# One scan chain over the chunks for all channel groups, and all states copied out at once

## The chip, the cores and the metric

One core of a Trainium2 chip. The metric is the device time of one execution in microseconds (us). A run gives the time of an execution; one execution is also taken by the hardware profiler, which lists the instructions of the five engines (TensorE, VectorE, ScalarE, GpSimd, SyncE) and the DMA transfers.

## What is computed

One layer of a backbone over 1024 latent tokens and 256 context tokens, width 1024. A mixer runs two groups of channels side by side, an output projection joins them, and a squared-ReLU MLP follows; both are post-normalised. The change lies in the second group of the mixer, the S5 part:

```python
def run(u, h0):
    bu = jnp.einsum('blgh,gph->blgp', u.astype(jnp.complex64), b_bar)
    a = jnp.broadcast_to(lam_bar, (1, u.shape[1]) + lam_bar.shape)
    h, h_fin = linear_scan(a, bu, h0, reverse)
    return jnp.einsum('blgp,ghp->blgh', h, c_mat).real, h_fin
h0 = jnp.zeros((u_ctx.shape[0], S5_GROUPS, S5_STATE), jnp.complex64)
y_ctx, h_fin = run(u_ctx, h0)
y_lat, _ = run(u_lat, h_fin)
```

64 groups of 16 channels each drive 64 complex diagonal states, forwards and backwards; the scan over the latent tokens starts from the last state of the context. A skip, a Gelu and a gated linear unit (GLU, `g * sigmoid(g @ w + b)`) follow.

## The kernel before

Tokens are taken in chunks of 8, so there are 32 chunks of context and 128 of latent tokens (`CC` = 32, `NCH` = 160), and the scan runs over chunks. Inside a chunk everything is matmuls with prepared operands. The 64 groups stand in eight channel tiles m = 0 to 7 of eight groups.

`s5_in` (line 590) makes the chunks' inputs to the scan: per group two matmuls on TensorE into PSUM, and copies of the result into the state tile, H0 for tiles 0 to 3 and H1 for tiles 4 to 7 (128 partitions x 160 chunks x real and imaginary x 32 groups). Partitions 0 to 63 hold the forward direction (line 603, ScalarE), 64 to 127 the backward one with the chunks reversed, in two copies for context and latent chunks (lines 605 and 606: VectorE for m < 4, ScalarE for the others).

`scan` (line 608), called for one half at a time, works on VectorE. It first brings the 32 context chunks together in five levels of a tree (tile sC), and then goes through 127 steps, one latent chunk after the other. A step has three instructions, all on line 47, a helper: sT (both products, 128 elements per partition), sU (their sum, 64) and the addition into H (64). Each needs the one before.

`s5_states` copies a tile's states, out of H in the order that the matmuls want, into h2: forwards on ScalarE (line 724), backwards on ScalarE for m < 4 and on VectorE for the others (line 725). When the four tiles of a half are copied, G0 or G1, the input of the GLU, takes the memory of H0 or H1. `s5_out` then does, per tile, 24 matmuls into two PSUM banks (lines 751 to 753, tile ps_so, two buffers), a Gelu on ScalarE (line 754, tile gs), eight transposes (ps_gt) and a split of the result into a high and a low part in G (line 762 ScalarE, line 763 VectorE through line 47). It loads mt, u2 and yf. The GLU's products (ps_gl) of the first two output tiles run along with it.

Between `s5_in` and `s5_out` TensorE has other work, which needs no scan: the gate projections `proj_gate` (ps_mm, evicted by a Gelu into ge) and the first half of the output projection (ps_wo). Their weights come as fp32 and are split on the way into a high part wh (ScalarE, line 98) and a low part wl (VectorE, line 47); the same is done to some of the inputs mh (mix_in).

The order of the instructions on each engine isn't the order of the code. A scheduler places them by its own costs of engines and transfers; each engine then works through its list in order, waiting where an operand isn't there. So the scan steps of both halves, weight splits and gate products are interleaved on VectorE.

Of the kernel before, what the change touches and what calls it, by code (L numbers as in the profile page):

```python
# [15 lines left out]
P = 128  # L16
# [25 lines left out]
def build(nc, tc, a, out):  # L42
# [541 lines left out]
    hp_ = [pool("h0", side="right", stack=hst)]  # L584
    sc = pool("sc", side="right", stack=hst)
    hp_.append(pool("h1", side="right", stack=hst))
    H = [p.tile([P, NCH, 2, GH], F32, tag="h", name=f"H{i}", bufs=1) for i, p in enumerate(hp_)]
# [4 lines left out]
    def s5_in(m):  # L592
        ub = inp.tile([P, 8, NCH], F32, tag="ub", name="ub", bufs=2)
        ld(ub, uscr[m].rearrange("t (c g) n -> (t c) g n", g=8))
        for q in range(2):
            xt = inp.tile([P, 4, 2, P], F32, tag="xt", name="xt", bufs=3)
            in_ld[m] = ld(xt, xscr[m, q])
            for g in range(4):
# [5 lines left out]
                cp = V.tensor_copy if m < 4 else S.copy  # L604
                cp(hv[64:128, :, 0:CC], ps[64:128, :, CC - 1::-1])
                cp(hv[64:128, :, CC:NCH], ps[64:128, :, NCH - 1:CC - 1:-1])

    def scan(hf):
        h = H[hf]
        hs = slice(hf * GH, (hf + 1) * GH)  # L610

# [10 lines left out]
        al = sc.tile([P, 2, 2, GH], F32, tag=f"al{hf}", name=f"al{hf}", bufs=1)  # L622
        V.tensor_copy(al[:, 0], a8[:, 0, 0:1, hs].to_broadcast([P, 2, GH]))
        V.tensor_copy(al[:, 1], a8[:, 0, 1:3, hs])
        for i in range(CC, NCH - 1):
            t = sc.tile([P, 2, 2, GH], F32, tag=f"sT{hf}", name="sT", bufs=2)
            tt(t, al, h[:, i - 1:i].to_broadcast([P, 2, 2, GH]), MUL)
            u = sc.tile([P, 2, GH], F32, tag=f"sU{hf}", name="sU", bufs=2)
            tt(u, t[:, 0], t[:, 1, ::-1, :], ADD)
            tt(h[:, i], u, h[:, i], ADD)  # L630
# [14 lines left out]
    for hf in range(2):  # L645
        for m in range(4):
            s5_in(4 * hf + m)
    inst.close()
    for m in range(8):
        proj_gate(m)  # L650
# [78 lines left out]
    def s5_states(m):  # L729
        h2 = h2s[m] = sop[m % 4 // 3].tile([P, 8, 2, CL], F32, tag="h2", name="h2", bufs=3 if m % 4 < 3 else 1)  # L730
        for q in range(2):
            starts(H[m // 4], h2[:, 4 * q:4 * q + 4], (m % 4) * 8 + 4 * q, V.tensor_copy if m >= 4 else S.copy)

    def s5_out(m):
        if m % 2 == 0:
            mtt[m // 2] = sop[1].tile([P, 16, P], F32, tag="mt", name="mt", bufs=2)
            kv = kpscr[m // 2].rearrange("m (g c) x -> c (m g) x", g=8)
            for t in range(T8):
                ld(mtt[m // 2][16 * t:16 * t + 16], kv[:, :, (8 - t) * 16:(8 - t) * 16 + P])
        mt = mtt[m // 2][:, 8 * (m % 2):8 * (m % 2) + 8]  # L740
# [24 lines left out]
    for hf in range(2):  # L765
        if hf == 0:
            scan(0)
# [696 lines left out]
```

## Time and profile before

| | us |
|---|---|
| runs: 1600.06, 1594.12, 1595.54; median | 1595.54 |
| profiled execution, its time | 1594.69 |
| its span in the trace | 1592.9 |
| TensorE (PE) busy | 1476.7 (93%) |
| VectorE (DVE) busy | 1256.8 (79%) |
| ScalarE (ACT) busy | 843.0 (53%) |
| scan steps sT, 254 on VectorE, mean 0.286 | 66.9 busy |

Busy times are sums over the whole span; an engine that is 79% busy can still be the one waited for in a stretch. Times in the rows are counted from the start of the span. A row of a timeline shows start and length of an instruction (or of several of one kind that follow each other, with their number), engine, line, what is written and what it is made from, and in brackets how long the engine had been idle before, and what ended that idle time. Instructions of one engine may overlap in part, so the distance between two starts, and not the length, tells what an instruction costs its engine.

### The profile page before, as it was taken

To read this page: it belongs to the slowest core of one execution; us is meant where nothing else is said; L and a number is where in the kernel's file an instruction comes from. 1 tells how busy PE (TensorE), PEld (TensorE's weight loads), DVE (VectorE), ACT (ScalarE), POOL (GpSimd) and SP (SyncE) were. 2 spreads that over 40 slices of the span, in tenths; PEclk is the share of its full clock that TensorE was granted. 3 is DMA by queue.
4 is the path that set the end of the run, shared out by engine and by line. 5 is a ranking of instruction groups with operands and counts; after the bars stand their busy time and mean duration, and the time that the engine had idled before them with its cause. 6 is when DMAs were issued, how large, how long until landed. Compare 5 with 4: busy or idle time off the path is not lost. (4 is left out here: it accounts for less than half of the span.)

```text
span 1592.9 us, 20440 instructions
## 1 busy us (share of the span) xinstructions
PE 1476.7 (93%) x7148; PEld 1202.4 (75%) x7148; DVE 1256.8 (79%) x2555; ACT 843.0 (53%) x1178; POOL 71.0 (4%) x141
## 2 busy tenths in 40 slices
PE   7899998999978999699999799989899899999997
PEld 2687777778756878598878677867788788888886
DVE  7899999998866989635978789778787566667877
ACT  4675656666795331954233576444555554344425
POOL 0000000000000000000000011111111000000000
PEclk9999999999999999799999999999999999999999
DMA  7623323323664752983768576777764786776703
GB/s 255 233 94 119 115 99 120 105 106 119 231 215 137 209 183 91 264 201 119 228 207 265 173 242 232 279 248 268 245 219 167 268 287 215 263 251 210 240 7 106
DMA packets 131382, 304.16 MB, mean 191 GB/s; under 512 B 16208, under 2 KB 47440, under 8 KB 129872
## 3 DMA queue, kind: packets, MB, share of 16 engines
q1 hardware_dynamic: 104048, 237.45, 46.9%
q0 software_dynamic: 13184, 47.72, 8.4%
q10 hardware_dynamic: 14048, 17.70, 3.1%
q8 instruction: 56, 0.92, 0.2%
q14 instruction: 46, 0.38, 0.1%
HBM read 219.52 MB, written 83.30 MB: 190 GB/s over the span
## 5 line engine op out<-in xcount | busy, mean ns | idle before, releaser
L98 ACT CAST wh<-wr 128x1024 fp32r<-128x1024 f32 x113 | 118.4, 1051 | 230.0 <-PE ps_m L1276 73.8
L47 DVE TENSOR_TENSOR wl<-wr,wh 128x1024 fp32r<-128x1024 f32 (+1 forms) x161 | 170.5, 1060 | 83.7 <-ACT wh L98 77.2
L1066 PE MATMUL ps_m<-xt,wh 128*128 128x512 f32 x512 | 160.7, 395 | 0.0
L1276 PE MATMUL ps_m<-bh,wh 128*128 128x512 f32 x392 | 153.7, 392 | 3.8 <-ACT bh L1238 3.7
L1276 PE MATMUL ps_m<-bl,wh 128*128 128x512 f32 x392 | 153.4, 391 | 0.5 <-DVE bl L47 0.5
L1276 PE MATMUL ps_m<-bh,wl 128*128 128x512 f32 x392 | 153.3, 391 | 0.0
L380 PE MATMUL ps_mm<-x0h,wh 128*128 128x512 f32 x352 | 140.3, 399 | 1.0 <-ACT wh L98 1.0
L380 PE MATMUL ps_mm<-x0h,wl 128*128 128x512 f32 x352 | 140.0, 399 | 0.9 <-DVE wl L47 0.9
L380 PE MATMUL ps_mm<-x0l,wh 128*128 128x512 f32 x352 | 140.0, 398 | 0.0
L1066 PEld LDWEIGHTS ps_m<-xt,wh 128*128 128x128 f32 x512 | 97.5, 191 | 21.2 <-issue 0.3
L1066 PE MATMUL ps_m<-xt,wl 128*128 128x512 f32 x256 | 101.9, 398 | 10.5 <-DVE wl L47 10.5
L1276 PEld LDWEIGHTS ps_m<-bh,wh 128*128 128x128 f32 x392 | 73.8, 188 | 20.6 <-ACT bh L1238 4.1
L1276 PEld LDWEIGHTS ps_m<-bl,wh 128*128 128x128 f32 x392 | 74.0, 189 | 16.6 <-DVE bl L47 1.0
L1276 PEld LDWEIGHTS ps_m<-bh,wl 128*128 128x128 f32 x392 | 74.0, 189 | 15.5
L675 PE MATMUL ps_wo<-ms,wh 128*128 128x512 f32 x256 | 81.7, 400 | 2.7 <-ACT ms L799 2.7
L1066 PE MATMUL ps_m<-x,wh 128*128 128x512 f32 x256 | 81.8, 400 | 1.0 <-ACT wh L1149 1.0
L380 PEld LDWEIGHTS ps_mm<-x0h,wl 128*128 128x128 f32 x352 | 67.2, 191 | 14.3 <-DVE wl L47 1.4
L380 PEld LDWEIGHTS ps_mm<-x0h,wh 128*128 128x128 f32 x352 | 67.1, 191 | 13.5 <-ACT wh L98 1.4
L380 PEld LDWEIGHTS ps_mm<-x0l,wh 128*128 128x128 f32 x352 | 67.1, 191 | 12.5
L47 DVE TENSOR_TENSOR sT<-al,H 128x128 f32<-128x128 f32 x254 | 66.9, 286 | 1.3
L1066 PEld LDWEIGHTS ps_m<-xt,wl 128*128 128x128 f32 x256 | 49.0, 191 | 23.6 <-DVE wl L47 13.4
L47 DVE TENSOR_TENSOR bl<-br,bh 128x1024 fp32r<-128x1024 f32 x49 | 59.5, 1218 | 2.2 <-ACT bh L1238 2.2
(352 smaller groups left out, 3696.2 us busy)
## 6 DMA issues: line engine op xcount, KB each, us to landing
wr<-in_w SPq DMA_DIRECT2D x79, 512.0 KB, 5.2
br<-hq SPq DMA_DIRECT2D x49, 512.0 KB, 5.0
mo<-in_ada_t SPq DMA_DIRECT2D x32, 512.0 KB, 4.1
hq<-hs POOLq DMA_DIRECT2D x14, 1024.0 KB, 8.2
wr<-in_w_in SPq DMA_DIRECT2D x24, 512.0 KB, 4.3
wr<-in_w_out SPq DMA_DIRECT2D x24, 512.0 KB, 4.5
xt<-xt ACTq DMA_DIRECT2D x16, 512.0 KB, 2.7
yd<-Y SPq DMA_DIRECT2D x16, 512.0 KB, 2.6
```

What stands on the lines that cost most here:

```text
L47: (eng or V).tensor_tensor(out=o, in0=x, in1=y, op=op)
L98: S.copy(hi, raw)
L380: PE.matmul(ps, w[:, ks], x, start=(k == 0 and c == 0), stop=(k == KT - 1 and c == 2))
L675: PE.matmul(ps, u[:, ks], v[:, js], start=(c == 0), stop=(c == 3 * KT - 1))
L1066: PE.matmul(ps, u[:, ks], v, start=(first and c == 0), stop=(last and c == 11))
L1276: PE.matmul(pss[m], w[:, 512 * k + P * m:512 * k + P * m + P], x[:, 512 * k:512 * k + 512], start=(q == 0 and k == 0 and c == 0), stop=(q ...
```

## The change

H0 and H1 become one tile H for all 64 groups. The context scan stays apart for each half and is called as soon as that half's inputs are there (`scan_context`). The 127 steps are done once, for both halves in one instruction each: sT has 256 elements per partition, sU and H 128. All eight tiles' states are then copied out, forwards on ScalarE, backwards on VectorE, and one tile G takes the place of H. In `s5_in` the backward copies are shared out in another way. For the memory that this takes, h2 has seven buffers in two pools, and `s5_out` loads mt per tile (it was per two tiles) and u2 and yf per half tile.

```diff
@@ -581,10 +581,10 @@
 
 
     hst, inst = ExitStack(), ExitStack()
-    hp_ = [pool("h0", side="right", stack=hst)]
+    hp_ = pool("h", side="right", stack=hst)
     sc = pool("sc", side="right", stack=hst)
-    hp_.append(pool("h1", side="right", stack=hst))
-    H = [p.tile([P, NCH, 2, GH], F32, tag="h", name=f"H{i}", bufs=1) for i, p in enumerate(hp_)]
+    HA = hp_.tile([P, 2, NCH, 2, GH], F32, tag="h", name="H", bufs=1)
+    H = [HA[:, i] for i in range(2)]
     inp = pool("inp", stack=inst)
 
     last_in, in_ld = {}, {}
@@ -601,14 +601,13 @@
                     last_in[m] = PE.matmul(ps[:, i, :], xt[:, g, i, :], ub[:, 4 * q + g, :], start=True, stop=True)
                 hv = H[m // 4].rearrange("p s r g -> p r s g")[:, :, :, (m % 4) * 8 + 4 * q + g]
                 S.copy(hv[0:64], ps[0:64])
-                cp = V.tensor_copy if m < 4 else S.copy
-                cp(hv[64:128, :, 0:CC], ps[64:128, :, CC - 1::-1])
-                cp(hv[64:128, :, CC:NCH], ps[64:128, :, NCH - 1:CC - 1:-1])
-
-    def scan(hf):
+                (V.tensor_copy if g % 2 else S.copy)(hv[64:128, :, 0:CC], ps[64:128, :, CC - 1::-1])
+                V.tensor_copy(hv[64:128, :, CC:NCH], ps[64:128, :, NCH - 1:CC - 1:-1])
+
+    def scan_context(hf):
+
         h = H[hf]
         hs = slice(hf * GH, (hf + 1) * GH)
-
         for q in range(5):
             d = 1 << q
             for o in range(0, CC, 16 * d):
@@ -619,15 +618,22 @@
                 tt(t[1], a8[:, q, 1:3, hs].unsqueeze(1).to_broadcast([P, n, 2, GH]), lo, MUL)
                 tt(hi, t[0], hi, ADD)
                 tt(hi, t[1][:, :, ::-1, :], hi, ADD)
-        al = sc.tile([P, 2, 2, GH], F32, tag=f"al{hf}", name=f"al{hf}", bufs=1)
-        V.tensor_copy(al[:, 0], a8[:, 0, 0:1, hs].to_broadcast([P, 2, GH]))
-        V.tensor_copy(al[:, 1], a8[:, 0, 1:3, hs])
+
+    def scan():
+
+        al = sc.tile([P, 2, 2, 2, GH], F32, tag="al", name="al", bufs=1)
+        for hf in range(2):
+            hs = slice(hf * GH, (hf + 1) * GH)
+            V.tensor_copy(al[:, 0, hf], a8[:, 0, 0:1, hs].to_broadcast([P, 2, GH]))
+            V.tensor_copy(al[:, 1, hf], a8[:, 0, 1:3, hs])
+        h = HA.rearrange("p f s r g -> p s f (r g)")
+        al = al.rearrange("p i f r g -> p i f (r g)")
         for i in range(CC, NCH - 1):
-            t = sc.tile([P, 2, 2, GH], F32, tag=f"sT{hf}", name="sT", bufs=2)
-            tt(t, al, h[:, i - 1:i].to_broadcast([P, 2, 2, GH]), MUL)
-            u = sc.tile([P, 2, GH], F32, tag=f"sU{hf}", name="sU", bufs=2)
-            tt(u, t[:, 0], t[:, 1, ::-1, :], ADD)
-            tt(h[:, i], u, h[:, i], ADD)
+            t = sc.tile([P, 2, 2, 2, GH], F32, tag="sT", name="sT", bufs=2)
+            tt(t.rearrange("p i f r g -> p i f (r g)"), al, h[:, i - 1].unsqueeze(1).to_broadcast([P, 2, 2, 2 * GH]), MUL)
+            u = sc.tile([P, 2, 2, GH], F32, tag="sU", name="sU", bufs=2)
+            tt(u, t[:, 0], t[:, 1, :, ::-1, :], ADD)
+            tt(h[:, i], u.rearrange("p f r g -> p f (r g)"), h[:, i], ADD)
 
 
     def proj_gate(m):
@@ -645,7 +651,9 @@
     for hf in range(2):
         for m in range(4):
             s5_in(4 * hf + m)
+        scan_context(hf)
     inst.close()
+    scan()
     for m in range(8):
         proj_gate(m)
     sost, mixst = ExitStack(), ExitStack()
@@ -727,30 +735,28 @@
     mtt, h2s = {}, {}
 
     def s5_states(m):
-        h2 = h2s[m] = sop[m % 4 // 3].tile([P, 8, 2, CL], F32, tag="h2", name="h2", bufs=3 if m % 4 < 3 else 1)
+        h2 = h2s[m] = sop[2 < m < 7].tile([P, 8, 2, CL], F32, tag="h2", name="h2", bufs=4 if 2 < m < 7 else 3)
         for q in range(2):
-            starts(H[m // 4], h2[:, 4 * q:4 * q + 4], (m % 4) * 8 + 4 * q, V.tensor_copy if m >= 4 else S.copy)
+            starts(H[m // 4], h2[:, 4 * q:4 * q + 4], (m % 4) * 8 + 4 * q, V.tensor_copy)
 
     def s5_out(m):
-        if m % 2 == 0:
-            mtt[m // 2] = sop[1].tile([P, 16, P], F32, tag="mt", name="mt", bufs=2)
-            kv = kpscr[m // 2].rearrange("m (g c) x -> c (m g) x", g=8)
-            for t in range(T8):
-                ld(mtt[m // 2][16 * t:16 * t + 16], kv[:, :, (8 - t) * 16:(8 - t) * 16 + P])
-        mt = mtt[m // 2][:, 8 * (m % 2):8 * (m % 2) + 8]
-        u2 = sop[1].tile([P, 8, CL], F32, tag="u2", name="u2", bufs=3)
-        ld(u2, uscr[m].rearrange("t (c g) n -> (t c) g n", g=8)[:, :, CC:NCH])
-        yf = sop[1].tile([P, 2, 2, 4, P], F32, tag="yf", name="yf", bufs=3)
-        ld(yf, yscr[m])
+        mt = sop[1].tile([P, 8, P], F32, tag="mt", name="mt", bufs=2)
+        kv = kpscr[m // 2][m % 2].rearrange("(g c) x -> c g x", g=8)
+        for t in range(T8):
+            ld(mt[16 * t:16 * t + 16], kv[:, :, (8 - t) * 16:(8 - t) * 16 + P])
         h2 = h2s[m]
         gs = sc.tile([P, T8, 8, 16], F32, tag="gs", name="gs", bufs=2)
         for s in range(2):
+            u2 = sop[1].tile([P, 4, CL], F32, tag="u2", name="u2", bufs=3)
+            ld(u2, uscr[m].rearrange("t (c g) n -> (t c) g n", g=8)[:, 4 * s:4 * s + 4, CC:NCH])
+            yf = sop[1].tile([P, 2, 4, P], F32, tag="yf", name="yf", bufs=4)
+            ld(yf, yscr[m][:, s])
             ps = psx.tile([P, 4, P], F32, tag="si", name="ps_so", bufs=2)
             for g in range(4):
                 gl = 4 * s + g
-                PE.matmul(ps[:, g, :], u2[:, gl, :], mt[:, gl, :], start=True, stop=False)
-                PE.matmul(ps[:, g, :], h2[:, gl, 0, :], yf[:, s, 0, g, :], start=False, stop=False)
-                PE.matmul(ps[:, g, :], h2[:, gl, 1, :], yf[:, s, 1, g, :], start=False, stop=True)
+                PE.matmul(ps[:, g, :], u2[:, g, :], mt[:, gl, :], start=True, stop=False)
+                PE.matmul(ps[:, g, :], h2[:, gl, 0, :], yf[:, 0, g, :], start=False, stop=False)
+                PE.matmul(ps[:, g, :], h2[:, gl, 1, :], yf[:, 1, g, :], start=False, stop=True)
             S.activation(gs[:, :, 4 * s:4 * s + 4].rearrange("n t g c -> n g t c"),
                          ps.rearrange("n g (t c) -> n g t c", t=T8), AF.Gelu_apprx_tanh)
         hl = glin[m]
@@ -762,19 +768,14 @@
             S.copy(hl[:, 0, HS[j]], pf)
             tt(hl[:, 1, HS[j]], pf, f(hl[:, 0, HS[j]]), SUB)
 
-    for hf in range(2):
-        if hf == 0:
-            scan(0)
-        for m in range(4 * hf, 4 * hf + 4):
-            s5_states(m)
-        if hf == 0:
-            scan(1)
-
-        g = hp_[hf].tile([P, 5, 2, NL], F32R, tag="h", name=f"G{hf}", bufs=1)
-        for m in range(4):
-            glin[4 * hf + m] = g[:, m]
-        for m in range(4):
-            s5_out(4 * hf + m)
+    for m in range(8):
+        s5_states(m)
+
+    gt = hp_.tile([P, 10, 2, NL], F32R, tag="h", name="G", bufs=1)
+    for m in range(8):
+        glin[m] = gt[:, m]
+    for m in range(8):
+        s5_out(m)
     sost.close()
     zst = ExitStack()
     zp = pool("zp", stack=zst)
```

The orders of the two kernels at three places. Names end in a buffer's number.

ScalarE in `s5_in`, second half of the groups, before:

```order
L603 COPY H1_3775<-ps_si_4043 64x2x160
L605 COPY H1_3775<-ps_si_4043 64x2x32
L606 COPY H1_3775<-ps_si_4043 64x2x128
L603 COPY H1_3775<-ps_si_4053 64x2x160
L605 COPY H1_3775<-ps_si_4053 64x2x32
L606 COPY H1_3775<-ps_si_4053 64x2x128
L603 COPY H1_3775<-ps_si_4059 64x2x160
L605 COPY H1_3775<-ps_si_4059 64x2x32
L606 COPY H1_3775<-ps_si_4059 64x2x128
```

and now:

```order
L603 COPY H_3771<-ps_si_4075 64x2x160
L603 COPY H_3771<-ps_si_4085 64x2x160
L604 COPY H_3771<-ps_si_4085 64x2x32
L98 CAST wh_5124<-wr_5122 128x1024
L642 ACTIVATE ge_5049<-ps_mm_5024 128x512
L603 COPY H_3771<-ps_si_4091 64x2x160
L98 CAST wh_5191<-wr_5189 128x1024
L603 COPY H_3771<-ps_si_4097 64x2x160
L604 COPY H_3771<-ps_si_4097 64x2x32
L603 COPY H_3771<-ps_si_4103 64x2x160
```

The long copy of the backward latent chunks (line 606 before) is no longer in ScalarE's list, and the short one stands behind every second group; two weight splits have come in between.

VectorE in the chain of steps, before, with both halves under way:

```order
L47 TENSOR_TENSOR sT_6131<-al1_6038,H1_3775 128x128
L47 TENSOR_TENSOR sU_5554<-sT_5552 128x64
L47 TENSOR_TENSOR sU_6133<-sT_6131 128x64
L47 TENSOR_TENSOR H0_3774<-sU_5554,H0_3774 128x64
L47 TENSOR_TENSOR H1_3775<-sU_6133,H1_3775 128x64
L47 TENSOR_TENSOR sT_5557<-al0_5344,H0_3774 128x128
L47 TENSOR_TENSOR sT_6136<-al1_6038,H1_3775 128x128
L47 TENSOR_TENSOR sU_5559<-sT_5557 128x64
L47 TENSOR_TENSOR sU_6138<-sT_6136 128x64
```

and now, with a weight split and a gate product between the instructions of two steps:

```order
L47 TENSOR_TENSOR sT_4395<-al_4280,H_3771 128x256
L47 TENSOR_TENSOR wl_5469<-wr_5466,wh_5468 128x1024
L47 TENSOR_TENSOR sU_4397<-sT_4395 128x128
L47 TENSOR_TENSOR ge_5317<-ge_5317 128x512
L47 TENSOR_TENSOR H_3771<-sU_4397,H_3771 128x2x64
L47 TENSOR_TENSOR sT_4400<-al_4280,H_3771 128x256
L47 TENSOR_TENSOR sU_4402<-sT_4400 128x128
L47 TENSOR_TENSOR H_3771<-sU_4402,H_3771 128x2x64
```

Two chains, with an instruction of the other between two of the one, have become one chain of instructions of double length.

ScalarE where the states are copied out and `s5_out` begins, before (H0 first, H1 later):

```order
L724 COPY h2_5997<-H0_3774 64x1024
L725 COPY h2_5997<-H0_3774 64x1024
L724 COPY h2_5997<-H0_3774 64x1024
L725 COPY h2_5997<-H0_3774 64x1024
L98 CAST wh_7228<-wr_7226 128x1024
L754 ACTIVATE gs_6690<-ps_so_6691 128x4x8x16
L754 ACTIVATE gs_6690<-ps_so_6705 128x4x8x16
L724 COPY h2_6883<-H1_3775 64x1024
L762 CAST G0_6676<-ps_gt_6719 128x512
L762 CAST G0_6676<-ps_gt_6726 128x512
L724 COPY h2_6883<-H1_3775 64x1024
L754 ACTIVATE gs_6737<-ps_so_6738 128x4x8x16
```

and now:

```order
L732 COPY h2_6016<-H_3771 64x1024 x2
L732 COPY h2_6021<-H_3771 64x1024 x2
L732 COPY h2_6026<-H_3771 64x1024 x2
L732 COPY h2_6031<-H_3771 64x1024 x2
L732 COPY h2_6036<-H_3771 64x1024 x2
L732 COPY h2_6041<-H_3771 64x1024 x2
L732 COPY h2_6046<-H_3771 64x1024 x2
L732 COPY h2_6051<-H_3771 64x1024 x2
L760 ACTIVATE gs_6066<-ps_so_6071 128x4x8x16
L760 ACTIVATE gs_6066<-ps_so_6089 128x4x8x16
L768 CAST G_6056<-ps_gt_6103 128x512
```

Before, the Gelu of the first tile stood behind the copies of the first half alone, and each copy of the second half behind a Gelu or a split of the first. Now the sixteen copies of all tiles stand in one piece ahead of the first Gelu.

## Rows read from the trace of the kernel before

**Rows 1.** Busy time by windows: engines PE, PEld, DVE, ACT, POOL; clock, DMA.

```profile
661.00:673.86 12.86, 0.00 (x1) 0.00 (x1) 1.75 (x2) 12.75 (x13) 1.13 (x2) 0.63 1.13 325
678.00:740.00 62.00, 62.00 (x466) 57.44 (x465) 18.95 (x24) 29.58 (x37) 0.00 (x0) 1.00 0.65 170
```

**Rows 2.** Waits of TensorE, 417 to 760 us: total, times, longest.

```profile
PE ps_si L601 <- ACT H L606: 13.1, 23, 0.7
PE ps_so L751 <- ACT gs L754: 13.0, 1, 13.0
```

**Rows 3.** Timeline of ScalarE around the copies of H0's states.

```profile
637.14 2.08 ACT L724 COPY h<-H 64x1024 f32<-64x1024 f32 x1 [6.20 <-DVE H L47]
...
670.32 1.92 ACT L725 COPY h<-H 64x1024 f32<-64x1024 f32 x1
672.26 1.04 ACT L98 CAST wh<-wr 128x1024 fp32r<-128x1024 f32 x1
673.21 1.08 ACT L754 ACTIVATE gs<-ps_so 128x512 f32<-128x512 f32 x2
```

**Rows 4.** Timeline: last step of H1's chain on VectorE, TensorE's restart.

```profile
659.45 0.23 DVE L47 TENSOR_TENSOR H<-sU,H 128x64 f32<-128x64 f32 x1
...
673.86 0.80 PE L751 MATMUL ps_so<-mt,u 128*128 128x128 f32 x2 [13.01 <-ACT gs L754]
```

**Rows 5.** Groups by line and shape, 400 to 760 us: busy, mean ns, idle before.

```profile
L47 DVE TENSOR_TENSOR sT<-al,H 128x128 f32<-128x128 f32 x254 | 66.9, 286 | 1.3
L47 DVE TENSOR_TENSOR H<-sU,H 128x64 f32<-128x64 f32 x254 | 49.7, 219 | 1.3
...
L724 ACT COPY h<-H 64x1024 f32<-64x1024 f32 x16 | 32.0, 2003 | 6.3 <-DVE H L47 6.2
...
L47 DVE TENSOR_TENSOR sC<-a,H 128x512 f32<-128x512 f32 x12 | 8.1, 697 | 22.9 <-ACT H L605 22.8
...
L47 DVE TENSOR_TENSOR mh<-mraw,mh 128x1024 fp32r<-128x1024 f32 x3 | 3.7, 1222 | 4.7 <-ACT mh L662 4.7
...
L47 DVE TENSOR_TENSOR H<-sC,H 128x256 f32<-128x256 f32 x4 | 1.7, 417 | 0.0
```

**Rows 6.** Timeline of VectorE: a gate product, and a split between two steps.

```profile
523.09 0.68 DVE L47 TENSOR_TENSOR ge<-ge 128x512 f32<-128x512 f32 x1
...
594.62 1.21 DVE L47 TENSOR_TENSOR wl<-wr,wh 128x1024 fp32r<-128x1024 f32 x1
595.76 0.21 DVE L47 TENSOR_TENSOR sU<-sT 128x64 f32<-128x64 f32 x1
```

**Rows 7.** Timeline of VectorE: copies of the first half, context scan, first step.

```profile
441.04 0.26 DVE L605 COPY H<-ps_si 64x64 f32<-64x64 f32 x1
441.16 0.59 DVE L606 COPY H<-ps_si 64x256 f32<-64x256 f32 x1
441.60 0.27 DVE L605 COPY H<-ps_si 64x64 f32<-64x64 f32 x1
...
445.19 1.34 DVE L47 TENSOR_TENSOR sC<-a,H 128x512 f32<-128x512 f32 x2
...
456.63 0.29 DVE L47 TENSOR_TENSOR sT<-al,H 128x128 f32<-128x128 f32 x1
```

**Rows 8.** Timeline of ScalarE: copies of the second half, beginning and end.

```profile
446.14 0.26 ACT L605 COPY H<-ps_si 64x64 f32<-64x64 f32 x1
446.25 0.60 ACT L606 COPY H<-ps_si 64x256 f32<-64x256 f32 x1
...
447.60 0.26 ACT L605 COPY H<-ps_si 64x64 f32<-64x64 f32 x1
...
491.08 0.63 ACT L606 COPY H<-ps_si 64x256 f32<-64x256 f32 x1
```

**Rows 9.** Timeline of VectorE: steps of one half alone, and in pairs.

```profile
457.48 0.29 DVE L47 TENSOR_TENSOR sT<-al,H 128x128 f32<-128x128 f32 x1
...
458.32 0.29 DVE L47 TENSOR_TENSOR sT<-al,H 128x128 f32<-128x128 f32 x1
...
586.66 0.48 DVE L47 TENSOR_TENSOR sT<-al,H 128x128 f32<-128x128 f32 x2
...
587.61 0.48 DVE L47 TENSOR_TENSOR sT<-al,H 128x128 f32<-128x128 f32 x2
```

**Rows 10.** DMA issues: KB each, median us to landing.

```profile
mt<-kp SPq DMA_DIRECT2D x32, 128.0 KB, 5.7
```

## The prediction

> **What bounds the kernel now.** I read the stretch from 417 to 760 us, where the S5 part lies, by windows first [rows 1]. TensorE is at work in all of 678 to 740 us and in none of 661 to 673.86: the one long hole in this stretch. The waits of TensorE over it [rows 2] name the reason: the first matmul of the second channel tile of s5_out waits 13.0 us for the Gelu of line 754, which must empty its PSUM bank. The ScalarE timeline [rows 3] tells why the Gelu is late. ScalarE copies the states of groups 0 to 31 out of H0, sixteen copies of 2.00 us [rows 5], begun when the chain of H0 ends at 637.1; the last starts at 670.32, the Gelu at 673.21, and TensorE goes on at 673.86 [rows 4]. The chain of H1 ends at 659.7 [rows 4] and holds nobody up: its copies lie between the Gelus of tiles 0 to 3 while TensorE is full. So this stretch ends by: chain of one half, its copies, Gelu. What the change does to 673.86 is what it does to the kernel, since the work behind is the same and TensorE is full there [rows 1].
>
> **The change, part by part.** The orders show it: the first Gelu now stands behind the copies of all eight tiles, and all copies behind the one chain of both halves. So the new time of resumption is: end of the input phase, context scan, chain, sixteen ScalarE copies, Gelu.
>
> *Input phase (s5_in).* The first half ends on VectorE at 445.19 [rows 7]. Of its copies VectorE loses half the short ones; loads and TensorE also held it back, so I take 446. In the second half ScalarE had three copies per group, 1.46 us from one to the next, and ended at 491.7 [rows 8]. It now loses the copy of 0.6 us and half of the short ones: about 0.8 us, 32 groups in 26 us. VectorE is longer now: per group 0.44 us for the long copy and half of 0.12 for the short one [rows 7], 32 x 0.50 = 16.0; in between stands the context scan of the first half, 445.19 to 456.63, 11.4 us; and three weight splits, 1.14 from start to start for a duration of 1.21 [rows 6], and two ge products, 0.60 by the same difference for 0.68 [rows 6]: 4.6. That is 32.0 us. With 2 us for waits between engines the phase ends at 446 + 34 = 480. Bounds: ScalarE alone would allow 472; no gain at all leaves 491.7.
>
> *Context scan of the second half.* 11.4 us again, with three ge and one split among it (2.9): the chain begins at 494.4. Before, VectorE idled 22.8 us in front of it [rows 5]; that idle goes.
>
> *The chain.* Before, a step of one half alone takes 457.48 to 458.32, 0.85 us [rows 9]: three instructions, each waiting for the one before. Two interleaved halves take 586.66 to 587.61, 0.95 us for the pair [rows 9]: the instructions of one half run in the other's latency. The merged step keeps the three waits and doubles the lengths. From 64 to 128 elements an instruction grows by 286 - 219 = 67 ns, from 128 to 256 by 417 - 286 = 131 [rows 5], so the step takes 0.85 + 0.131 + 2 x 0.067 = 1.115 us, and 127 steps 141.6 us. Halving the number of instructions thus buys nothing over the pairs: 0.95 against 1.115. It gains only over the stretches in which one half runs alone, some 14 steps ahead of the context scan of H1 and some 25 at the end.
>
> Among the steps stand 13 weight splits, 3 splits of mix inputs and 9 ge. Between two dependent steps such an instruction costs its own spacing, less the latency that it covers, (2 x 0.85 - 0.95) / 6 = 0.13 us as in the pair: 1.14 - 0.13 = 1.01 and 0.60 - 0.13 = 0.47, together 16.2 + 4.2 = 20.4. The mix splits wait, as before, for inputs that come back through DRAM: 4.7 us [rows 5]. So the chain ends at 494.4 + 141.6 + 20.4 + 4.7 = 661.1, for both halves, 1.4 us behind the old end of H1 and 24 us behind that of H0, the one that counted.
>
> *Copies.* All sixteen on ScalarE now start there: 16 x 2.00 = 32.0 us. VectorE's sixteen, of the same shape, lie beside them. Nothing is left to cover them: by then TensorE has only the first tile's 24 matmuls. With the Gelu and the restart (0.65, from 673.21 to 673.86) TensorE goes on at 693.8.
>
> *What is hidden.* TensorE's gate and output projections can end some 20 us sooner (ahead of the last input matmul stand 54 gate matmuls where 23 stood, and the stalls on ScalarE in the input phase go), but that only lengthens the hole. The weight splits they need stand early enough in the chain, so they add no stall. ScalarE is freed of eight copies between the Gelus behind the hole; TensorE was full there, so that is worth nothing.
>
> *More and smaller loads.* mt, u2 and yf now come in 48 more transfers, with buffers for about two tiles in place of three. A tile takes TensorE 9.4 us (673.9 to 740 for seven); a transfer of mt lands 5.7 us after issue [rows 10]. The first three tiles lie ready during the hole. For the other five I take 0; the upper bound is 2 us each, 10 us; a gain is excluded, since TensorE did not wait for them.
>
> **Sum.** 693.8 - 673.9 = +19.9 us. The profiled execution took 1594.7 us (span 1592.9 and 1.8 around it), 0.9 below the median of 1595.5. 1594.7 + 19.9 = **1615 us**.
>
> **A rule against a row.** The rows give a tensor_tensor 0.219 us at 64 elements and 0.286 at 128 [rows 5]: about 0.15 us fixed, whatever the length. The Trainium skill ("VectorE: DVE Perf Modes", sections on the TRN2 errata and on rules for kernel authors) says that VectorE exposes this latency between instructions, that one large tile pays it once, and advises fewer instructions. It calls for the merge. The pair's 0.95 us [rows 9] disagrees: six instructions with durations of 1.45 us in all lie in it, so between independent ones much of the fixed part is already hidden.
>
> **Rivals.**
> *A, faster: length is free in a waiting chain.* If the wait alone set the step, the merged one would take 0.85 us: 127 x 0.265 = 33.7 us less, TensorE on at 660.1, 1581. For it: the same three waits. Against: the rows on length [rows 5]. It decides (over 0.5%, 8 us, about what a measurement here can tell from no change) below 0.895 us per step.
> *B, same: each instruction pays its fixed part in full and nothing else.* Then a merged step is 0.417 + 2 x 0.286 = 0.99 us with no gap: 16 us less than my chain, 1599. Against: a single step takes 0.85 us [rows 9] for durations of 0.72, so a waiting instruction starts 0.04 us behind the end of the last. This is what the skill's rule of the paragraph above comes to at best.
> *C, slower still: the loads of s5_out set its pace.* With fewer buffers each tile from the fourth on waits some 2 us: 1625. For it: eight mt transfers are issued per tile, not per two. Against: a tile's buffers are free nearly a tile and a half before its successor needs them.
> *D, the input phase gains nothing.* If loads or TensorE hold it, it ends at 491.7 and all moves by 12 us: 1627. For it: the same loads now have to come in less time. Against: up to 491 ScalarE's copies followed each other without a gap [rows 8], and nothing else in that half was full.
>
> **Chances.** Forecast 0.60, A 0.07, B 0.13, C 0.12, D 0.08. Faster by over 0.5%: 0.07 (A). Within 0.5%: 0.14 (B, and the low end of the forecast). Slower: 0.79. Range 1600 to 1627: the low end is the forecast with the input phase at its bound of 472 and no wait of the mix splits (12.7 us less, 1602) and B's neighbourhood; the high end is C and D, each alone. A lies outside, and C with D.
>
> **What would show it.** Right: sT at about 0.42 us and three instructions per 1.10 to 1.13 us; one hole of TensorE of 50 us or more, but for 24 matmuls, that ends near 694 us on the Gelu; sixteen ScalarE copies without a gap from about 661; no idle of VectorE in the input phase. Wrong: steps under 0.95 us, copies that begin before 645, a Gelu between the copies, or new DMA waits in s5_out.

## The result, and the profile after

The changed kernel takes 1636.2 us (median of 4 runs, 1631.8 to 1637.5) where the kernel before took 1594.8: ratio 1.0249, interval 1.0218 to 1.0280. Slower was forecast, but by 20 us and not by 41; the range ended at 1627. The profiled execution took 1635.7 us with a span of 1633.9, 41.0 us more than the span before.

Windows of the changed kernel (columns as in [rows 1]):

```profile
452.00:492.00 40.00, 35.04 (x183) 27.49 (x182) 37.52 (x80) 29.12 (x53) 0.00 (x0) 1.00 0.72 241
...
661.00:678.00 17.00, 3.85 (x18) 3.85 (x19) 15.94 (x36) 5.82 (x4) 0.00 (x0) 0.50 0.00 0
678.00:703.00 25.00, 4.72 (x32) 4.53 (x32) 13.85 (x12) 24.53 (x15) 0.00 (x0) 0.64 0.31 85
...
740.00:778.00 38.00, 34.30 (x251) 30.46 (x250) 5.73 (x9) 9.17 (x17) 0.00 (x0) 1.00 0.60 180
```

The hole of TensorE, 12.86 us before [rows 1], now reaches from 644 to 703 with one tile's matmuls in it, first at a granted clock of 0.50 (1.2 GHz). What is new stands in the last line: in the stretch behind the hole, where TensorE was busy without a break [rows 1], it is idle for 3.7 of 38 us. The waits of TensorE, 400 to 900 us (total, times, longest), name both:

```profile
PE ps_so L758 <- ACT h L732: 29.7, 1, 29.7
PE ps_gt L766 <- ACT gs L760: 24.4, 7, 20.3
PE ps_si L601 <- DVE H L605: 11.1, 8, 7.3
```

The first is the wait for the chain and the first copies; of the second, 20.3 us are the wait for the first Gelu, which answers to the 13.0 us of [rows 2], and the rest is a short wait in six more tiles. The third lies in the input phase, 7.3 us of it at its start. ScalarE's timeline shows where that comes from, and the end of the hole:

```profile
426.00 0.69 ACT L603 COPY H<-ps_si 64x320 f32<-64x320 f32 x1 [4.85 <-DMA hs<-ii]
...
672.18 29.38 ACT L732 COPY h<-H 64x1024 f32<-64x1024 f32 x16 [26.03 <-DVE H L47]
701.46 1.06 ACT L760 ACTIVATE gs<-ps_so 128x512 f32<-128x512 f32 x2
```

The first copy into H waits for a store (of the last head's sum, tile ii, through GpSimd's queue). Before, it came at 420.92 and waited for something else:

```profile
420.92 1.26 ACT L603 COPY H<-ps_si 64x320 f32<-64x320 f32 x2 [0.95 <-DMA ge<-hs]
```

The sixteen copies follow without a gap, as forecast, and the Gelu behind them. VectorE's timeline has copies between the instructions of the first context scan, the last copy of the input phase (it ends at 491.6), and the first step of the chain:

```profile
453.98 0.69 DVE L47 TENSOR_TENSOR H<-sC,H 128x512 f32<-128x512 f32 x1
454.70 0.59 DVE L605 COPY H<-ps_si 64x256 f32<-64x256 f32 x1
455.31 0.69 DVE L47 TENSOR_TENSOR H<-sC,H 128x512 f32<-128x512 f32 x1
...
491.01 0.62 DVE L605 COPY H<-ps_si 64x256 f32<-64x256 f32 x1
...
505.36 0.42 DVE L47 TENSOR_TENSOR sT<-al,H 128x256 f32<-128x256 f32 x1
```

The chain, in VectorE's groups between 500 and 672 us and in its timeline:

```profile
L47 DVE TENSOR_TENSOR sT<-al,H 128x256 f32<-128x256 f32 x127 | 53.9, 425 | 4.0
L47 DVE TENSOR_TENSOR H<-sU,H 128x128 f32<-128x128 f32 x127 | 37.1, 292 | 4.1
```

```profile
600.39 0.42 DVE L47 TENSOR_TENSOR sT<-al,H 128x256 f32<-128x256 f32 x1
...
601.50 0.43 DVE L47 TENSOR_TENSOR sT<-al,H 128x256 f32<-128x256 f32 x1
```

1.11 us per step, against 0.95 for the pair in [rows 9]. TensorE's restart, and two of the tiles behind it:

```profile
702.58 1.97 PE L766 MATMUL ps_gt<-ident,gs 128*128 128x128 f32 x8 [20.28 <-ACT gs L760]
...
734.25 1.09 PE L766 MATMUL ps_gt<-ident,gs 128*128 128x128 f32 x8 [0.69 <-ACT gs L760]
735.58 0.74 PE L702 MATMUL ps_gl<-G,wh 128*128 128x512 f32 x2 [0.24 <-ACT G L768]
...
744.72 1.09 PE L766 MATMUL ps_gt<-ident,gs 128*128 128x128 f32 x8 [0.69 <-ACT gs L760]
```

One tile takes 744.72 - 734.25 = 10.47 us, and in each TensorE stands twice: for the tile's own Gelu, ahead of the transposes, and for G, ahead of the GLU's products.

So the 41.0 us are: restart at 702.58 and not 673.86 [rows 4], 28.7; from there to the last transposes 74.6 us (end 777.21) where it was 64.8 (end 738.66), 9.8; the rest of the program 856.7 for 854.2, 2.5. This rest lay between 850.0 and 858.9 us in the eleven traces of experiments made from the changed kernel, so I give it no cause.

### The profile page after: what moved, and what is told of

It reads as the page before. It is cut to its first block, busy times and chain, and to the rows that moved or that the text cites. A ratio compares the mean times of both kernels' runs of the same rounds, so it can differ in the third digit from the quotient of the medians.

```text
span 1633.9 us, 20142 instructions
## 1 busy us (share of the span) xinstructions
PE 1481.4 (91%) x7148; PEld 1205.0 (74%) x7148; DVE 1284.4 (79%) x2214; ACT 811.0 (50%) x1138; POOL 70.9 (4%) x141
## 5 line engine op out<-in xcount | busy, mean ns | idle before, releaser
L1067 PE MATMUL ps_m<-xt,wl 128*128 128x512 f32 x256 | 100.9, 395 | 9.9 <-DVE wl L47 9.9
L47 DVE TENSOR_TENSOR G<-ps_gt,G 128x512 fp32r<-128x512 f32 x16 | 10.4, 687 | 68.6 <-ACT G L768 68.4
```

The lines of the kernel that those rows point to most:

```text
L47: (eng or V).tensor_tensor(out=o, in0=x, in1=y, op=op)
L1067: PE.matmul(ps, u[:, ks], v, start=(first and c == 0), stop=(last and c == 11))
```

## The experiments

My theory after the traces: four costs on one path. The merged chain (1.11 us a step for 0.95), the copies behind it, the order that the scheduler makes of s5_out with the small loads, and the late start of the input phase. The rivals are that a cost is hidden by another, or that the pace of s5_out has another cause. Ratios are to the kernel before, run on the same chip; the changed kernel's is 1.0249. The difference of two ratios carries the uncertainty of both, here 6 to 8 us; where a difference is no larger, the traces decide.

### The chain as two chains

```diff
-            t = sc.tile([P, 2, 2, 2, GH], F32, tag="sT", name="sT", bufs=2)
...
+            for hf in range(2):
+                ts_.append(sc.tile([P, 2, 2, GH], F32, tag=f"sT{hf}", name="sT", bufs=2))
+                tt(ts_[hf], al[hf], H[hf][:, i - 1:i].to_broadcast([P, 2, 2, GH]), MUL)
...
+            for hf in range(2):
+                tt(H[hf][:, i], us_[hf], H[hf][:, i], ADD)
```

> The changed kernel with its one tile H kept, but the chain's step issued as six instructions, three for each half, interleaved as in the kernel before. Theory (three instructions that wait for one another pay for their doubled length, six in pairs hide the latency): a step goes from 1.11 to 0.95 us, 127 steps end about 20 us sooner (near 652 in place of 672.1), and 1636 becomes about 1615. Rival (the steps are set by what stands between them, weight splits and waits): less than 5 us, 1631 or more.

Ratio 1.0797, interval 1.0770 to 1.0825: neither theory. The waits of TensorE, 470 to 640 us, tell why:

```profile
PE ps_mm L380 <- DVE wl L47: 120.7, 2, 119.5
```

Written ahead of the projections, two chains were placed by the scheduler with all their paired steps ahead of the weight splits. The merged chain stands in the same place and has splits in between. I take the reason to be that two chains always have a ready instruction and the merged one waits for itself; no run shows it. So the next run moves the call of the scan behind the projections:

```diff
     inst.close()
-    scan()
...
+    scan()
     for m in range(8):
         s5_states(m)
```

> The changed kernel with its one tile H kept, and the chain's step issued as six instructions, three for each half; this time the chains stand behind the gate and output projections in the program, so that the scheduler lets VectorE's weight splits go ahead of them. (Where they stood ahead, in the first run with two chains, VectorE did nothing but the chains for 120 us and TensorE waited for a weight split.) Theory (three waiting instructions pay for their doubled length, six in pairs hide the latency): 0.95 us per step in place of 1.11, the chain's end near 652 in place of 672.1, 1636 becomes about 1616. Rival (the length of the steps does not set the chain's end): 1631 or more.

Ratio 1.0152 (1.0130 to 1.0174), 15.5 us less than the changed kernel. VectorE's timeline:

```profile
636.06 0.35 DVE L47 TENSOR_TENSOR H<-sU,H 128x64 f32<-128x64 f32 x2
...
637.01 0.35 DVE L47 TENSOR_TENSOR H<-sU,H 128x64 f32<-128x64 f32 x2
...
658.40 1.29 DVE L734 COPY h<-H 64x1024 f32<-64x1024 f32 x1
```

0.95 us per pair, the chain done at 658.4 and not 672.1, 13.8 us sooner. Not all of the 20 us arrive: VectorE waited 12.0 us here for mix inputs and gate values, 4.9 in the changed kernel. The theory holds: the merge costs some 14 to 15 us. The call stands in another place too; a merged chain in that place was not run, so that the gain is the pairing's rests on the step, 0.95 for 1.11 us.

### The order of s5_out

First the kernel before, with the loads of s5_out alone as in the changed kernel (mt per tile, u2 and yf per half, their buffers):

```diff
-        u2 = sop[1].tile([P, 8, CL], ..., bufs=3)
-        yf = sop[1].tile([P, 2, 2, 4, P], ..., bufs=3)
+            u2 = sop[1].tile([P, 4, CL], ..., bufs=3)
+            yf = sop[1].tile([P, 2, 4, P], ..., bufs=4)
```

> The kernel before, with the loads of s5_out cut and buffered as in the changed one, and nothing else changed. Theory (with these loads the scheduler puts a tile's transposes right behind its own matmuls, and TensorE then waits for the Gelu in every tile, as in the changed kernel, 0.9 us shown and some more around it): a tile takes 10.5 us in place of 9.1, seven tiles 8 to 10 us more, 1595 becomes about 1604, and the waits of TensorE are for ScalarE, not for a DMA. Rival 1 (the pace of the changed kernel comes from the copies being gone from between the Gelus, or from the one tile G): no change, 1595. Rival 2 (the loads are late): the same loss, with waits for DMA.

Ratio 1.0104 (1.0082 to 1.0126), 16.6 us, more than the 8 to 10 expected. The waits of TensorE, 640 to 770 us, and its timeline:

```profile
PE ps_gt L758 <- ACT gs L752: 23.9, 8, 17.4
PE ps_gl L694 <- ACT G L760: 4.8, 7, 1.2
```

```profile
700.50 1.09 PE L758 MATMUL ps_gt<-ident,gs 128*128 128x128 f32 x8 [0.69 <-ACT gs L752]
702.82 1.45 PE L694 MATMUL ps_gl<-G,wh 128*128 128x512 f32 x5 [1.23 <-ACT G L760]
...
711.95 1.09 PE L758 MATMUL ps_gt<-ident,gs 128*128 128x128 f32 x8 [0.69 <-ACT gs L752]
```

No DMA is waited for. The scheduler's order changed with the loads: transposes directly behind a tile's own 24 matmuls, where before matmuls of the next tile, or products of the GLU, stood between. A tile takes 11.45 us here, since the second half's copies also stand between Gelu and G.

Then the changed kernel, with only the order undone:

```diff
+            half[m, s] = mm           # last matmul of a half tile
             for t in range(4):
-                PE.transpose(pt[:, t, :], ...)
+                with after(half.get((m + 1, 0))):
+                    PE.transpose(pt[:, t, :], ...)
```

> The changed kernel, with the transposes of a tile in s5_out held until the first twelve matmuls of the next tile are issued; loads, chain and copies are those of the changed kernel. Theory (the order, with the transposes right behind a tile's own matmuls, lets TensorE wait for the Gelu in every tile): a tile takes 9.1 to 9.4 us in place of 10.47, six to seven tiles 7 to 9 us, 1636 becomes about 1628. Rival (the pace is set by the small loads or by the way Gelu, transposes and G hang together): a wait for a DMA or ScalarE takes its place, 1634 or more.

Ratio 1.0208 (1.0178 to 1.0238), 6.5 us less, though the two intervals overlap. The trace decides: a tile takes 9.61 us, and the last transposes end 98.5 us after the chain in place of 105.1:

```profile
723.72 1.04 PE L773 MATMUL ps_gt<-ident,gs 128*128 128x128 f32 x8
...
733.33 1.04 PE L773 MATMUL ps_gt<-ident,gs 128*128 128x128 f32 x8
```

The wait for each tile's Gelu is gone with the loads unchanged; the theory holds.

### The start of the input phase

Two runs write the last head's sum elsewhere, so that H does not lie over a tile whose store is running:

```diff
-        tt(it[0][:, NC:NT], it[0][:, NC:NT], it[1][:, NC:NT], ADD)
+        hv = it[0][:, NC:NT] if h < 7 else ...   # a weight buffer; then the spent xc
+        tt(hv, it[0][:, NC:NT], it[1][:, NC:NT], ADD)
```

> The changed kernel, with one thing undone: the last head's sum is written to a weight buffer, so that the single tile H no longer lies over a tile whose store through GpSimd's queue is still running. Theory (that store holds the start of the input phase): the first copy into H comes near 421 us in place of 426.0, and the chain's end (672.1) and the restart of TensorE (702.6) come about 5 us sooner; 1636 becomes about 1631. Rival (the input phase is set by VectorE's work or the loads): the start comes sooner, the phase still ends near 491.6, and the time stays at 1636.

Ratio 1.0453 (1.0425 to 1.0481): it tells nothing of the store, since the scheduler moved three gate projections ahead of the input phase, which began at 457.

> The changed kernel, with one thing undone: the last head's sum is written over the spent tile xc, which H does not cover, and stored from there; the order of TensorE is that of the changed kernel, row for row. (The run before this one wrote it to a weight buffer, and the scheduler then put three gate projections ahead of the input phase.) Theory (the store through GpSimd's queue holds the start of the input phase): the first copy into H comes near 421 us in place of 426.0, the chain's end (672.1) and the restart of TensorE (702.6) about 5 us sooner, 1636 becomes about 1631. Rival (the phase is set by VectorE's work or the loads): it starts sooner and still ends near 491.6, 1636.

Ratio 1.0245 (1.0223 to 1.0267), unchanged, and no verdict: H waits for this store too.

```profile
427.57 0.69 ACT L603 COPY H<-ps_si 64x320 f32<-64x320 f32 x1 [5.30 <-DMA hs<-xc]
```

Two more send the same store through another queue, first SP's:

```diff
-        (nc.sync if h < 7 else G).dma_start(out=d, ...)
+        nc.sync.dma_start(out=d, ...)          # then: (nc.sync if h < 7 else S)
```

> The changed kernel, with the last head's sum stored through SP's queue in place of GpSimd's; TensorE's order is that of the changed kernel. The run with the sum in xc left the wait in place (5.3 us for the store, the scheduler still had H wait for it), so it told nothing of its price. Rows: stores of this size through SP land 2.6 us after issue, the one through GpSimd 4.9. Theory (the wait for this store is the start of the chain of work that ends at TensorE's restart, us for us): the first copy into H comes 2 to 3 us sooner, the chain's end and the restart as well, 1636 becomes 1633 or 1634. Rival (the delay is absorbed in the input phase): the start moves, the chain's end does not, 1636.

Ratio 1.0272 (1.0251 to 1.0293), 4 us more, but overlapping with the changed kernel's. ScalarE's timeline, and the waits of TensorE from 410 to 500 us:

```profile
430.16 0.70 ACT L603 COPY H<-ps_si 64x320 f32<-64x320 f32 x1 [8.26 <-PE ps_si L601]
...
678.63 1.92 ACT L732 COPY h<-H 64x1024 f32<-64x1024 f32 x1 [25.10 <-DVE H L47]
```

```profile
PE ps_si L601 <- DMA xt<-xt: 9.8, 1, 9.8
```

On SP the store stands ahead of loads of ub and xt. The start comes 4.2 us later than in the changed kernel's trace, the state copies 6.4. Part of this is spread: with the store through GpSimd's queue the start lay between 424.8 and 429.0 us in the traces of the changed kernel and five of its experiments (419.2 to 423.2 in five traces of the kernel before and its experiments).

> The changed kernel, with the last head's sum stored through ScalarE's queue; TensorE's order is that of the changed kernel. The run through SP's queue made the start later, not sooner: 430.2 for 426.0, since the store stood ahead of a load of xt there and TensorE waited 9.8 us for it; the chain's end and the restart followed by 6.4 us each. Theory (the start of the input phase passes on to the end us for us): with a landing of about 2.7 us in place of 4.9 the first copy into H comes near 424, and 1636 becomes 1633 or 1634. Rival (another wait takes its place, for a load or for the queue): the start stays at 426 or later, 1636 or more.

Ratio 1.0222 (1.0190 to 1.0255), within the interval of the changed kernel, and the rival was right: this store takes as long through ScalarE's queue, and the start stays in that spread.

```profile
421.84 0.34 ACTq L462 DMA_DIRECT2D hs<-ii  x1
...
427.36 0.69 ACT L603 COPY H<-ps_si 64x320 f32<-64x320 f32 x1 [2.77 <-DMA hs<-ii]
```

So a later start is passed on: in the seven traces with the merged chain and these copies of the input phase, the chain ends 246.1 to 248.4 us after the first copy, whether that comes at 426.0 or, in the first run of this section, at 456.9. A start without the wait was not brought about, and its worth, some 5 us, is argued from rows, not shown.

### The copies of the input phase

```diff
-                (V.tensor_copy if g % 2 else S.copy)(hv[64:128, :, 0:CC], ...)
-                V.tensor_copy(hv[64:128, :, CC:NCH], ...)
+                cp = V.tensor_copy if m < 4 else S.copy    # both copies, as before
```

> The changed kernel, with the copies of the input phase as before: VectorE has both backward copies in the first half, ScalarE in the second. Theory (in the changed kernel VectorE is full through the second half, with the copies and the first context scan, so that moving copies to it gains little): the input phase ends near 497 in place of 491.6, VectorE idles again ahead of the second context scan, which then runs without copies between; the chain begins 2 to 5 us later, and 1636 becomes 1638 to 1641. Rival (the step as the prediction had it, the redistribution is worth 12 us): 1646 or more.

Ratio 1.0333 (1.0304 to 1.0362): 13.4 us slower than the changed kernel. My new theory fell, and the price that the prediction put on the step (12 us) came out, though not the way to it. VectorE's timeline, second context scan and first step:

```profile
496.29 1.30 DVE L47 TENSOR_TENSOR sC<-a,H 128x512 f32<-128x512 f32 x2 [34.19 <-ACT H L605]
...
513.45 0.42 DVE L47 TENSOR_TENSOR sT<-al,H 128x256 f32<-128x256 f32 x1
```

The phase ends 5 us later, and the chain begins 8 us later (505.36 in the changed kernel), since gate products and splits have piled up behind ScalarE's copies and fall into the context scan. The other 5.6 us come in the chain, which has one split and two gate products more among its steps and more waits for them.

The same edit made to the kernel before, alone:

> The kernel before, with the copies of the input phase alone as in the changed one; chains, state copies and loads of before. The run with both kinds of copies had the first chain end at 647.3 (637.1 before) and TensorE reach s5_out at 644.9 (651.6 before). Theory (VectorE's longer work in the second half delays the first chain; ScalarE's sixteen copies of 2.00 us stand behind it): the chain ends near 647, copies near 679, TensorE goes on near 681 in place of 673.9, and 1595 becomes about 1602; the gain of the run with both lies in the state copies moved to VectorE. Rival (the relief of ScalarE in the input phase is the gain itself): 1590 or less.

Ratio 1.0046 (1.0021 to 1.0070). ScalarE's and TensorE's timelines (of the shortest of ten executions, 1596.3 us):

```profile
640.09 1.94 ACT L723 COPY h<-H 64x1024 f32<-64x1024 f32 x1 [24.00 <-DVE H L47]
```

```profile
675.69 0.80 PE L750 MATMUL ps_so<-mt,u 128*128 128x128 f32 x2 [21.08 <-ACT gs L753]
```

The output projections end sooner, but the first chain ends 3 us later than before (637.14, [rows 3]); with sixteen copies behind it TensorE restarts later too, by 1.8 us. The median has come to the 1602 of the theory, but the trace has neither its chain's end (647) nor its restart (681), and the ten executions lie between 1596.3 and 1613.0. Most of the 7 us is thus unexplained.

### The state copies

```diff
-    ..., V.tensor_copy if m >= 4 else S.copy)     # before: backward copies of m < 4 on ScalarE
+    ..., V.tensor_copy)
```

> The kernel before, with one part of the change: the backward copies of the first half's states go to VectorE too. Theory (the 13.0 us wait of TensorE is for sixteen ScalarE copies behind the first chain): ScalarE has eight, done near 655, the Gelu follows the matmuls of the first tile at 661, TensorE goes on near 662 in place of 673.9, and 1595 becomes about 1583. VectorE's eight copies of 1.2 us delay the second chain by 10 us, which is hidden. Rival (the scheduler places VectorE's copies so that the first chain or the second half's states become late): TensorE waits elsewhere, and the time is 1590 or more.

Ratio 0.9985 (0.9968 to 1.0001), not the 12 us. The timelines of ScalarE and TensorE:

```profile
673.26 1.92 ACT L724 COPY h<-H 64x1024 f32<-64x1024 f32 x1 [9.23 <-DVE H L47]
675.09 1.05 ACT L762 CAST G<-ps_gt 128x512 fp32r<-128x512 f32 x2
```

```profile
675.72 1.73 PE L694 MATMUL ps_gl<-G,wh 128*128 128x512 f32 x2 [6.07 <-ACT G L762]
```

The 13 us wait is gone: TensorE's first transposes come at 664.1 (675.7 before). Then it stands for G: VectorE's eight copies delay the second chain to 673, and a copy of its states stands ahead of the cast to G in ScalarE's queue. The rival was right: the wait has moved.

Both kinds of copies together, two chains:

> The kernel before, with two parts of the change and no merged chain: the copies of the input phase as in the changed kernel (the long one always VectorE's, the short ones in turns), and the backward state copies all VectorE's. Theory (VectorE's 22.8 us of idle ahead of the second context scan are filled, so both chains end some 8 to 10 us sooner, and ScalarE's eight copies are done before TensorE reaches s5_out): the 13.0 us wait shrinks to under 4, and 1595 becomes 1583 to 1587. Rival (VectorE's longer work in the second half delays the first chain as much as the rest gains): the first chain ends near 645, the time is 1592 or more.

Ratio **0.9945 (0.9918 to 0.9972)**, faster than either kernel. The waits of TensorE, 640 to 760 us (of one of the longest of five executions, 1592.6 us):

```profile
PE ps_so L750 <- ACT gs L753: 9.8, 1, 9.8
PE ps_so L751 <- ACT h L723: 4.3, 2, 3.9
```

The wait does not shrink to 4 us as the theory had it. The first chain ends at 647.3, as the rival had it, but TensorE reaches s5_out at 644.8 (651.8 before) and comes to its last transposes at 732.2 (738.7). So the time is that of the theory and the end of the first chain that of the rival; that TensorE's earlier arrival brings the gain is read from this one trace.

In the changed kernel, four of ScalarE's copies given to VectorE:

> The changed kernel, with four of ScalarE's sixteen state copies given to VectorE (the second forward copy of every odd tile): twelve of about 1.83 us against twenty of 1.23 us. Theory (the copies lie bare between the chain's end and the first Gelu, and the slower engine's sum counts): ScalarE ends 22 us after the chain in place of 29.3, VectorE 24.6, TensorE goes on about 5 us sooner, 1636 becomes about 1631. Rival (the Gelu or G waits for something else in this stretch): 1635 or more.

Ratio 1.0216 (1.0179 to 1.0254), overlapping with the changed kernel's; its ScalarE timeline decides:

```profile
675.23 22.11 ACT L732 COPY h<-H 64x1024 f32<-64x1024 f32 x12 [26.14 <-DVE H L47]
697.24 1.07 ACT L760 ACTIVATE gs<-ps_so 128x512 f32<-128x512 f32 x2
```

The Gelu comes 22.0 us after the chain in place of 29.3, and the last transposes end 100.9 us after it in place of 105.1: of 7.3 us 4.2 are left there. The copies lie bare on the path.

### Three costs undone together

Two chains, transposes held, and the last store through SP, then through ScalarE:

> The changed kernel with three of its costs undone together: the chain as two interleaved chains behind the projections, the transposes of s5_out held behind the next tile's first matmuls, the last store through SP. One tile H, the copies, G and the loads stay. Theory (the costs lie one behind the other on the path and add up: 16 to 17 us of the chain, 7 of the order, 2 of the store): 1636 becomes about 1610, and what is left over before is the states' copies behind both chains. Rival (they cover one another, since the stretch is set by something else once one of them is gone): 1615 or more.

> The changed kernel with the chain as two interleaved chains behind the projections, the transposes held behind the next tile's first matmuls, and the last store through ScalarE's queue. The run before, with that store through SP, gave 1.0079 of the kernel before, with a start of the input phase at 431.7. Theory (the costs add up; the start was 7 us later there than it need be): 1636 less 16 for the chain, 7 for the order and 2 for the store, about 1610 less what the start gives back, 1603 to 1608. Rival (the start is absorbed once the chain is short): 1611 as before.

Ratios 1.0079 (1.0052 to 1.0106) and 1.0063 (1.0037 to 1.0090): 27 and 30 us of the 41 are gone. Chain and order add up: alone they gave back 15.5 and 6.5. The third cost was not undone: the first copy into H comes at 431.7 and 428.9, and the ratios, 2.5 us apart, do not tell theory from rival for the earlier start (in the traces, 2.9 us at the start are 4.3 at the chain's end). So that late start is left over before; the rest is in the waits of TensorE, 640 to 800 us, of the second:

```profile
PE ps_so L760 <- ACT gs L764: 16.0, 1, 16.0
PE ps_so L761 <- ACT h L733: 11.3, 1, 11.3
```

Both are for the copies behind two chains that end together.

## Why the prediction was right, and where wrong

The time lay above the range because two steps of the prediction failed: the end of the input phase, and the loads of s5_out, which it put at nothing. What bounds the kernel, the chain and the copies came out.

**What bounds it: right.** The restart of TensorE follows chain, sixteen copies and Gelu, and 28.7 of the 41.0 us are its delay. The prediction also took the restart for the whole change, since TensorE was full behind it; that failed, by the loads (below).

**Chain: right.** From 505.36 to 672.14 are 166.8 us; 141.6 + 20.4 + 4.7 = 166.7 was forecast, with 1.115 us a step. That halving the instructions buys nothing was tested: with pairs the kernel gained 15.5 us, and the chain ended 13.8 us sooner. The advice of the Trainium skill ("VectorE: DVE Perf Modes", rules for kernel authors) to lower the number of instructions fails here: 127 steps of three cost more than 127 of six. Rivals A and B are out.

**Context scan and copies: nearly right.** 13.9 us for 14.3; the first Gelu 29.3 us after the chain for 32.0, with 1.1 and not 0.65 to the restart.

**Input phase: wrong by 11.6 us.** "I take 446" and "the phase ends at 480"; it ended at 491.6. The first half ended at 452.8. Of those 6.8 us, 5.1 are the start at 426.0 for 420.9: I had looked at what the copies cost and not at what the first write into a larger tile waits for, which the profile after shows. The rest is ScalarE, which with half of the short copies is busy 24.9 of 26 us there. The second half took 38.9 us and not 34. VectorE was busy 37.5 of 40 us, and ScalarE waited 8.3 us for banks that VectorE empties, so VectorE sets the pace, as I had it; "2 us for waits between engines" was about right. The mis-sized term is the price of its copies, 16.0 us: from start to start they took 21.8, the few waits included, 0.60 us for the long one and not 0.44. My price came from the densest stretch of the kernel before [rows 7]; over its whole first half a long copy took 0.55 from start to start, and one that stands between instructions of the context scan takes 0.61 (454.70 to 455.31). What moving the copies is worth, 13.4 us between old and new copies for the 12 forecast, agrees by luck: the end of the phase moved by 5 us only, the rest came in context scan and chain. Rival D's time came true, though not for its reason.

**Loads of s5_out: wrong by 9.8 us.** "For the other five I take 0". I priced the loads as loads, and no load is waited for. But the scheduler answers to them with another order, and with it TensorE's 9.4 us per tile, which I took as given (9.1 at the full clock: the transposes of two tiles before, at 683.07 and 701.31, lie 18.24 us apart), became 10.47; seven tiles at 1.35 us more are 9.5. That the loads alone, sizes and buffers together, do this is shown in the kernel before (16.6 us there), and that it is the order in the run with the transposes held. "A gain is excluded" was right; the upper bound of 10 us held by luck, since its reason, late loads, was wrong.

Restart 8.8 us later than forecast, s5_out 9.8, the rest 2.5: these are the 21 us that were missing. The range took in C and D each alone; what came were the times of both.

## What to carry to other kernels

Two dependent chains that are interleaved already fill each other's latency (0.95 us for two steps, 0.85 for one [rows 9]); before they are merged, compare the merged step (its waits kept, its lengths doubled) with the paired one, and ask what waited for the first chain alone. When a tile grows or buffers are cut, read in the new order two things ahead of any duration: what the first write into the tile waits for, and whether consumers (here transposes) have moved closer to their producers. Work moved to an idle engine pays where the next wait behind it moves as well: in the kernel before, the move of the input copies alone lost 0.46%, that of the state copies alone gained nothing clear of the noise, and both together gained 0.55%.

## What the runs showed of the hardware that I had not expected

The DMA issues (KB each, us to landing): two lines of the changed kernel, then one of the run that stored the last head's sum through ScalarE's queue, and one of the run that stored it through SP's.

```profile
hs<-ii SPq DMA_DIRECT2D x4, 512.0 KB, 2.6
hs<-ii POOLq DMA_DIRECT2D x1, 512.0 KB, 4.9
```

```profile
hs<-ii ACTq DMA_DIRECT2D x1, 512.0 KB, 5.3
```

```profile
hs<-ii SPq DMA_DIRECT2D x1, 512.0 KB, 2.9
```

The last head's store is slow through ScalarE's queue as well as through GpSimd's; through SP it lands nearly as fast as the four earlier ones of the same size. There it was issued ahead of the loads of ub and xt, which then came late; through the other two queues, loads that SP had issued just before were under way beside it. So GpSimd's queue alone is not the reason. Whether it is the loads beside the store was not tried.

The state copies took 1.83 us from one to the next where only forward ones followed each other (29.38 us for sixteen, the last of 1.92). I had taken 2.00 [rows 5], a mean duration and no distance; of such copies one starts 0.09 us before the last ends. The duration also differs: in [rows 3] the first, beside VectorE's chain, has 2.08, the last, behind it, 1.92. That the chain is the reason was not tested.
